# Sixteen conditioning products of a decoder layer, moved from the merge into the mixing stage

## The chip, the cores and the metric

The kernel runs on one core of a Trainium2 chip (trn2). The metric is the device time of one execution in microseconds (us), the median of several runs. Before the change it is 793.3 us.

## The reference

One decoder layer for 512 tokens of width 1024, in float32. A per-sequence vector c conditions it: `mod = silu(c) @ w_ada + b_ada` gives six vectors of 1024 values, shift, scale and gate for each of the two halves of the layer.

```
h = rmsnorm(x, g_pre_mix) * (1 + sc1) + sh1
qa, ka, va, qb, kb, vb, qi, ki, wi, gate_a, gate_b = split(h @ w_in)
mixer a: an indexer picks 128 keys for each query; softmax attention over them
mixer b: stick-breaking attention, a scan over the keys
y = (sigmoid(gate_a) * (oa @ w_up_a) + sigmoid(gate_b) * (ob @ w_up_b)) @ w_out
x = x + ga1 * rmsnorm(y, g_post_mix)
h = rmsnorm(x, g_pre_ffn) * (1 + sc2) + sh2
x = x + ga2 * rmsnorm(relu(h @ w_ff1)**2 @ w_ff2, g_post_ffn)
```

Each mixer has 8 heads of 64. The change concerns two of the six vectors: ga1, the gate of the first half (used after the product with w_out), and sc2, the scale ahead of the MLP.

## The kernel before

Every product with float32 weights is made of three matmuls (`mm3`): weights and activations are each split into a high part (`hi`, by ScalarE, L113) and a low part (`lo`, by VectorE, L114), and high x high, high x low and low x high are summed. A weight tile is 128 x 1024 (512 KB). It is loaded by SyncE's queue into one of three buffers "st" (`stage`, L107 to L110), then split into one of four buffers "whi" and "wlo" (`wload`). Tokens stand in four tiles of 128.

The conditioning vectors are not made by matmuls. w_ada is stored transposed, so that one load of 128 x 1024 (`ada[j]`, j from 0 to 47) holds the weights of 128 outputs. VectorE multiplies it with silu(c), which stands as a row in all partitions (tile "cb"), and sums along the row: `ada_dot` (L213), one column of `mod`. Eight such products make one of the six vectors. `ada_cols(j)` is a load into "st" and this product. For ga1 (j = 16 to 23) and sc2 (j = 32 to 39) a small product with a norm gain follows (`gated_gain`, L134, and `scaled_gain`, L131). `silu_rows(pool)` loads c as a row into "cb" of a pool, takes its sigmoid on ScalarE (L161) and the product on VectorE (L162).

The stages in order of time:

- start (to about 57 us): sh1 and sc1, the first norm, the first tiles of w_in.
- mixing (about 57 to 325 us): `main_stream` makes the remaining projections, and generators (`indexer`, `attend`, `prep_a`) are stepped beside it, one `tick()` for each yield of the main stream, then alone until all are done. A step yields the number of ticks until its next one. The indexer ends with 16 rounds of the 8 largest values (L411, L412) and then writes the mask of selected keys (L416), on which the softmax of mixer a (`rows_a`, L468 to L476) waits.
- merge: for m = 0 to 7, one tile of gate_b (24 matmuls), the two up-projections (24 matmuls, into "s" banks), sigmoids, products and sum on ScalarE and VectorE, and the split of the result. After each m stand `LATE[m]` conditioning products.
- w_out, second norm, and the MLP (w_ff1, then w_ff2 with fewer products by a scheme of sums).

Outside of the start and of the last stage (`manual_schedule`) the order of each engine's queue is not that of the program text: a planner that knows modelled costs orders it ahead of time, and of what its model has ready it takes first what stands first in the text. On the chip each queue is then carried out as ordered. Loads stand on SyncE's queue in the same way.

Pools are stacked: the pool "tmp" (`tp`) of the mixing stage takes the place of the pool of the start stage, and the pool of the merge (`mp`) that of "tmp". The merge has its own `silu_rows(mp)`, so its "cb" is loaded when the mixing is over.

Of the kernel before, what the change touches and what calls it, by code (L numbers as in the profile page):

```python
# [7 lines left out]
F32 = mybir.dt.float32  # L8
# [6 lines left out]
P = 128  # L15
D = 1024
L = 512
NT = L // P
KT = D // P
# [23 lines left out]
A11, S1, S3, S2, A12, A22 = range(6)  # L43
EARLY = 4
WOB = 4
LATE = (0, 3, 4, 4, 4, 4, 4, 1)
HF_ACT = 0
EVAC = 1
EVAC_A = 3
# [16 lines left out]
def layer_kernel(tc, x, ada, vecs, c_row, rope, w_first, w_v, w_b, w_a, w_gate, w_up, w_out, w_ff1, w_ff2, w_right, out):  # L66
    nc = tc.nc
    es = ExitStack()
    with es:
        edge = es.enter_context(tc.tile_pool(name="edge", bufs=1, side="right"))  # L70
        per = es.enter_context(tc.tile_pool(name="per", bufs=1))
# [3 lines left out]
        def uid(name):  # L75
            cnt[0] += 1
            return f"{name}_{cnt[0]}"
# [25 lines left out]
        g2 = per.tile([P, KT], F32, name="g2")  # L103
# [3 lines left out]
        def stage(src, w=D):  # L107
            st = per.tile([P, D], F32, name=uid("st"), tag="st", bufs=3)
            nc.sync.dma_start(st[:, :w], src)
            return st  # L110
# [19 lines left out]
        def scaled_gain(dst, j, g0):  # L130
            nc.vector.scalar_tensor_tensor(dst, mod[:, j:j + 1], 1.0, vec[:, g0:g0 + 1], op0=ALU.add, op1=ALU.mult)  # L131

        def gated_gain(i, j, g0):
            nc.vector.tensor_tensor(ga[:, i:i + 1], mod[:, j:j + 1], vec[:, g0:g0 + 1], op=ALU.mult)  # L134
# [22 lines left out]
        def silu_rows(pool, sg=None):  # L157
            dst = pool.tile([P, D], F32, name=uid("cb"), tag="cb")
            sg = pool.tile([P, D], F32, name=uid("cs"), tag="cs") if sg is None else sg
            nc.sync.dma_start(dst, c_row.to_broadcast([P, D]))  # L160
            nc.scalar.activation(sg, dst, AF.Sigmoid)  # L161
            nc.vector.tensor_tensor(dst, dst, sg, op=ALU.mult)  # L162
            cb[:] = [dst]
# [32 lines left out]
        def slot(name, dt=F32, a=4):  # L196
            t = up.tile([P, 2048], dt, name=uid(name), tag="u8", bufs=6)
            return t.rearrange("p (a b) -> p a b", a=a)
# [13 lines left out]
        def ada_dot(j, st):  # L212
            nc.vector.tensor_tensor_reduce(out=st, in0=st, in1=cb[0], scale=1.0, scalar=vec[:, j:j + 1],  # L213
                                           op0=ALU.mult, op1=ALU.add, accum_out=mod[:, j:j + 1])

        def ada_cols(j):
            ada_dot(j, stage(ada[j]))
# [72 lines left out]
        tp = t_es.enter_context(tc.tile_pool(name="tmp", bufs=1, side="right"))  # L290
# [30 lines left out]
        def k_parts(src):  # L321
            s = tp.tile([P, NT, 3, HD], F32R, name=uid("ks"), tag="ks")
            split(s[:, :, 0, :], s[:, :, 1, :], src)
            nc.scalar.activation(s[:, :, 2, :], s[:, :, 0, :].bitcast(F32), AF.Copy)
            return s
# [7 lines left out]
        def turned(dst, s, i, t0=0):  # L333
            ps = bank("tr", F32R)
            for t in range(t0, NT):
                nc.tensor.transpose(ps[:, t * P:(t + 1) * P], s[:, t, i:i + 2].rearrange("p a d -> p (a d)"), identr)
            evac(dst[:, t0 * P:], ps[:, t0 * P:].bitcast(F32))
# [8 lines left out]
        mask = tp.tile([P, 1280], BF16, name="mask")  # L346
# [7 lines left out]
        tens = {}  # L354

        def spawn(gen, delay=0):
            tasks.append([now[0] + delay, gen])
# [11 lines left out]
        def indexer():  # L369
            do_rope(kw[:, :, None, :HD], 1)  # L370
            s = k_parts(kw[:, :, :HD])
            do_rope(qi[:, :NT - 1].rearrange("p t (h d) -> p t h d", h=NH), NH, 1)
            yield 2
            kk = tp.tile([P, 2, L], F32R, name="kTi")
            for i in range(2):
                turned(kk[:, i], s, i)
            head = lambda h: q_parts(qi[:, :NT - 1, h * HD:(h + 1) * HD])
            s = head(0)
            yield 2
            prev = None  # L380
            for h in range(NH + 1):
                q = None
                if h < NH:
                    q = tp.tile([P, L], F32R, name=uid("qTi"), tag="qTi", bufs=2)
                    turned(q, s, 0, 1)
                    if h + 1 < NH:
                        s = head(h + 1)
                    yield 1
                if prev is not None:
                    for b in range(1, NT):  # L390
                        n = (b + 1) * P
                        ps = scores(prev, kk, b)
                        r = row("rel")
                        nc.scalar.activation(r[:, :n], ps[:, :n], AF.Relu)
                        dst = isc[:, ISC0[b]:ISC0[b] + n]
                        w = kw[:, b, HD + h - 1:HD + h]
                        if h == 1:
                            nc.vector.tensor_scalar(dst, r[:, :n], w, None, op0=ALU.mult)
                        else:
                            nc.vector.scalar_tensor_tensor(dst, r[:, :n], w, dst, op0=ALU.mult, op1=ALU.add)  # L400
                    yield IDX_GAP
                prev = q
            for b in range(1, NT):
                dg = isc[:, ISC0[b] + b * P:ISC0[b] + (b + 1) * P]
                nc.gpsimd.affine_select(out=dg, in_=dg, pattern=[[-1, P]], compare_op=ALU.is_ge,
                                        fill=FILL, base=0, channel_multiplier=1)
            for i in range(TOPK // 8):
                for b in range(1, NT):
                    cur = isc[:, ISC0[b]:ISC0[b] + (b + 1) * P]
                    m8 = small(8)  # L410
                    nc.vector.max(out=m8, in_=cur)  # L411
                    nc.vector.match_replace(out=cur, in_to_replace=m8, in_values=cur, imm_value=SENT)  # L412
                    yield TOP_GAP[b - 1]
            for b in range(1, NT):
                n = (b + 1) * P
                nc.vector.tensor_scalar(mask[:, MSK0[b]:MSK0[b] + n], isc[:, ISC0[b]:ISC0[b] + n],  # L416
                                        -3.3e38, OFF, op0=ALU.is_gt, op1=ALU.mult)
            tens["mask"] = True
# [32 lines left out]
        def attend(key, v_src, rows, lag, gap, close):  # L451
            for hp in range(NH // 2):
                while f"{key}{hp}" not in tens:
                    yield 1
                yield QK_LAG
                pT = [pt_tile(e) for e in range(2)]
                for b in range(NT):
                    spawn(unit(hp, b, tens[f"{key}{hp}"], v_src, rows, pT, lag, close))
                    yield gap[b]
# [19 lines left out]
        def rows_b(q, kk, b):  # L479
# [8 lines left out]
            nc.vector.tensor_tensor(be[:, :n - 1], be[:, :n - 1], a[:, 1:n], op=ALU.mult)  # L488
            return be


        srcs = [(w_v[g, i, :, :(k1 - k0) * VREST], (k1 - k0) * VREST) for g in range(2) for i, (k0, k1) in enumerate(V_CUTS)]
        feeds = {"b": iter(w_b[i] for i in range(8)), "g": iter(w_gate[i] for i in range(8)), "a": iter(w_a[i] for i in range(8))}
# [125 lines left out]

        tens["vb"] = slot("vb")  # L620
        tens["sga"] = [slot("sga") for _ in range(2)]
        spawn(indexer())
        spawn(attend("b", tens["vb"], rows_b, LAG_B, GAP_B, close_b))
        spawn(attend("a", va, rows_a, LAG_A, GAP_A, close_a))
        for _ in main_stream():
# [25 lines left out]
        gsl = slot("mrg")  # L651
        mz = mp.tile([P, LINE // 4], F32, name="mz")[:, 0:1]
        nc.vector.memset(mz, 0.0)
        late = iter([base + k for base in (16, 32, 24) for k in range(KT)])
        for m in range(KT):
            pg = drain(cols_T(wnext()))
            sgb, ta = gsl[:, 2 * (m % 2)], gsl[:, 2 * (m % 2) + 1]
            nc.scalar.activation(sgb, pg, AF.Sigmoid)
            hi, lo = wnext()
            pa, pb = bank("s"), bank("s")  # L660
            for ps, oh, ol, c0 in ((pb, obh, obl, 512), (pa, oah, oal, 0)):
                for k in range(4):
                    cs = slice(c0 + k * P, c0 + (k + 1) * P)
                    mm3(ps, hi[:, cs], lo[:, cs], oh[k], ol[k], k == 0, k == 3)
            nc.vector.tensor_tensor(sgb, pb, sgb, op=ALU.mult)
            sga = tens["sga"][m // 4][:, m % 4]
            nc.scalar.activation(sga, sga, AF.Sigmoid, bias=mz)
            nc.vector.tensor_tensor(ta, pa, tens["sga"][m // 4][:, m % 4], op=ALU.mult)
            nc.vector.tensor_tensor(sgb, sgb, ta, op=ALU.add)
            split(mgh[m], mgl[m], sgb)  # L670
            for _ in range(LATE[m]):
                j = next(late)
                ada_cols(j)
                if j >= 32:
                    scaled_gain(g2[:, j - 32:j - 31], j, 32 + j)
                elif j < 24:
                    gated_gain(j - 16, j, 40 + j)
        u_es.close()
        h_es.close()

# [29 lines left out]
        for k in range(KT):  # L710
            if k < WOB:
                wo.append(wnext())
            else:
                st = stage(w_out[k])
# [410 lines left out]
```

## Time and profile before

| what | value |
|---|---|
| runs | 795.06, 793.3, 790.36 us; median 793.3 us |
| the profiled execution | 792.72 us, of which the span is 790.9 us |
| TensorE (PE) busy | 765.3 us, 97% of the span |
| VectorE (DVE) busy | 593.3 us, 75% |
| ScalarE (ACT) busy | 415.2 us, 53% |
| GpSimd (POOL) busy | 28.2 us, 4% |
| granted TensorE clock | 0.997 |
| conditioning loads into "st" | 32 of 512 KB, of which 24 for the merge |

The span runs from the first to the last instruction of the program. An engine's busy time is the time in which it carries out instructions; "PEld" is TensorE's loading of stationary weights, which overlaps its matmuls. A number after "x" counts instructions. In a timeline, a square bracket gives the idle time of the engine before an instruction and what ended it.

### The profile page before, as it was taken

What the parts mean: (1) busy time and instruction counts of PE and PEld (TensorE: products, weight loads), DVE (VectorE), ACT (ScalarE), POOL (GpSimd) and SP (SyncE); (2) the same over time, 40 slices, a digit from 0 to 9 for tenths busy, and PEclk for the clock granted to TensorE, in tenths of its full rate; (3) what the DMA queues carried; (4) which work ended last, traced back from release to release, by engine and by line L of the source; (5) the groups of instructions that cost most, each with busy time, mean ns of one, the idle gap of its engine ahead of it and who ended that gap; (6) DMA issues with size and microseconds to landing.
All of it is one profiled execution on the core that took longest, in us unless ns stands there. A gap on an engine that the chain in (4) does not pass through costs nothing.

```text
span 790.9 us, 10885 instructions
## 1 busy us (share of the span) xinstructions
PE 765.3 (97%) x4014; PEld 638.5 (81%) x4014; DVE 593.3 (75%) x1112; ACT 415.2 (53%) x752; POOL 28.2 (4%) x44
## 2 busy tenths in 40 slices
PE   6999999998899999999999999999999999999996
PEld 5889978667889877787778898888888878888885
DVE  6876799999966768688875875655645588888966
ACT  6545567654445758632245763232332367768852
POOL 0000000000000000000000000000000011151000
PEclk9999999999999999999999999999999999999999
DMA  9943211113122121177785155344431289899502
GB/s 359 389 122 106 73 37 54 55 53 107 46 89 80 56 65 43 53 249 259 253 278 210 36 187 174 131 139 153 142 105 63 71 202 226 192 208 261 190 1 107
DMA packets 32598, 111.18 MB, mean 141 GB/s; under 512 B 3872, under 2 KB 3872, under 8 KB 32544
## 3 DMA queue, kind: packets, MB, share of 16 engines
q1 hardware_dynamic: 28224, 99.44, 36.2%
q0 software_dynamic: 4176, 11.01, 8.1%
q8 instruction: 31, 0.51, 0.2%
q14 instruction: 23, 0.19, 0.1%
q10 hardware_dynamic: 144, 0.03, 0.0%
HBM read 108.38 MB, written 2.10 MB: 140 GB/s over the span
## 4 chain that ended last, share of the span: by engine, by line
PE 74%; DVE 15%; DMA 6%; ACT 2%; issue 2%; SPq 0%; DVEq 0%; ACTq 0%
PE mm L140 25%; PE s L140 19%; PE o L140 7%; PE s L859 6%; PE mm L859 5%; PE tr L859 5%; DMA st<-in_ada_dram 3%; DVE a L486 3%; DVE wlo L114 2%; DVE isc L412 2%; DVE sm L411 2%; DMA st<-in_w_up_dram 2%; PE tr L430 2%; DVE be L488 1%; PE tr L140 1%
## 5 line engine op out<-in xcount | busy, mean ns | idle before, releaser
L113 ACT ACTIVATE whi<-st 128x1024 fp32r<-128x1024 f32 (+3 forms) x102 | 102.2, 1005 | 161.2 <-DMA st<-in_w_up_dram 43.6
L114 DVE TENSOR_TENSOR wlo<-st,whi 128x1024 fp32r<-128x1024 f32 (+3 forms) x102 | 117.3, 1153 | 55.3 <-ACT whi L113 55.0
L140 PE MATMUL mm<-hTh,whi 128*128 128x512 f32 x192 | 78.2, 407 | 0.1
L140 PE MATMUL mm<-hTh,wlo 128*128 128x512 f32 x192 | 75.3, 392 | 0.0
L140 PE MATMUL mm<-hTl,whi 128*128 128x512 f32 x192 | 75.1, 391 | 0.0
L140 PE MATMUL mm<-whi,hTh 128*128 128x256 f32 (+2 forms) x208 | 62.7, 308 | 0.0
L213 DVE CUSTOM_DVE_ANT_0 st<-st,cb,vec 128x1024 f32<-128x1024 f32 x32 | 40.9, 1283 | 28.6 <-DMA st<-in_ada_dram 28.6
L140 PE MATMUL mm<-wlo,hTh 128*128 128x256 f32 (+2 forms) x208 | 60.6, 297 | 0.0
L140 PE MATMUL mm<-whi,hTl 128*128 128x256 f32 (+2 forms) x208 | 60.5, 297 | 0.0
L140 PE MATMUL s<-h2h,whi 128*128 128x512 f32 (+1 forms) x120 | 43.4, 361 | 0.0
L140 PE MATMUL s<-h2l,whi 128*128 128x512 f32 (+1 forms) x120 | 43.3, 361 | 0.0
L140 PE MATMUL s<-h2h,wlo 128*128 128x512 f32 (+1 forms) x120 | 43.3, 361 | 0.0
L140 PEld LDWEIGHTS mm<-hTh,wlo 128*128 128x128 f32 x192 | 36.0, 188 | 7.7
L140 PEld LDWEIGHTS mm<-hTh,whi 128*128 128x128 f32 x192 | 36.2, 189 | 6.6 <-DVE qT L524 0.3
L140 PEld LDWEIGHTS mm<-hTl,whi 128*128 128x128 f32 x192 | 36.2, 188 | 6.2
L140 PEld LDWEIGHTS mm<-wlo,hTh 128*128 128x128 f32 x208 | 40.1, 193 | 1.1
L140 PEld LDWEIGHTS mm<-whi,hTl 128*128 128x128 f32 x208 | 40.0, 192 | 0.6
L140 PEld LDWEIGHTS mm<-whi,hTh 128*128 128x128 f32 x208 | 39.6, 193 | 0.4
L859 PE MATMUL s<-whi,ah 128*128 128x512 f32 x100 | 36.1, 390 | 0.3 <-ACT whi L113 0.3
L140 PE MATMUL s<-kT,qT 128*128 128x256 f32 (+2 forms) x128 | 30.9, 346 | 2.1 <-ACT be L485 1.8
L879 POOL DMA_DIRECT2D wn<-in_w_right_dram x13 | 11.4, 876 | 582.2 <-DVE ub L898 532.6
L812 DVE TENSOR_TENSOR ub<-ub 128x512 f32<-128x512 f32 (+1 forms) x36 | 22.4, 627 | 10.8 <-ACT ub L811 10.8
(356 smaller groups left out, 1976.1 us busy)
## 6 DMA issues: line engine op xcount, KB each, us to landing
st<-in_w_ff_dram SPq DMA_DIRECT2D x50, 512.0 KB, 3.8
st<-in_ada_dram SPq DMA_DIRECT2D x32, 512.0 KB, 3.9
sa<-in_ada_dram SPq DMA_DIRECT2D x16, 512.0 KB, 8.1
st<-in_w_gate_dram SPq DMA_DIRECT2D x16, 512.0 KB, 3.4
ld<-in_w_ff_dram SPq DMA_DIRECT2D x14, 512.0 KB, 4.7
wn<-in_w_right_dram POOLq DMA_DIRECT2D x13, 512.0 KB, 5.5
st<-in_w_first_dram SPq DMA_DIRECT2D x8, 512.0 KB, 8.5
st<-in_w_b_dram SPq DMA_DIRECT2D x8, 512.0 KB, 3.3
```

Of the source, the lines that this page charges most:

```text
L113: nc.scalar.activation(dst_hi, src, AF.Copy)
L114: nc.vector.tensor_tensor(dst_lo, src, dst_hi.bitcast(F32), op=ALU.subtract)
L140: nc.tensor.matmul(o, lhsT, rhs, start=start, stop=stop)
L213: nc.vector.tensor_tensor_reduce(out=st, in0=st, in1=cb[0], scale=1.0, scalar=vec[:, j:j + 1], op0=ALU.mult, op1=ALU.add, accum_out=mod[:, ...
L411: nc.vector.max(out=m8, in_=cur)
L412: nc.vector.match_replace(out=cur, in_to_replace=m8, in_values=cur, imm_value=SENT)
L430: nc.tensor.transpose(tr[:, j * P:(j + 1) * P], ps[e][:, j * P:(j + 1) * P], ident)
L486: nc.vector.tensor_tensor_scan(a[:, n - 1::-1], a[:, n - 1::-1], zero.to_broadcast([P, n]), 1.0, op0=ALU.mult, op1=ALU.add)
L488: nc.vector.tensor_tensor(be[:, :n - 1], be[:, :n - 1], a[:, 1:n], op=ALU.mult)
L812: nc.vector.tensor_tensor(u, u, u, op=ALU.mult)
L859: nc.tensor.matmul(acc[i], s[:, ts], m[:, cs], start=f, stop=l, skip_group_check=onto)
L879: nc.gpsimd.dma_start(nw[p], w_right[p], accum_op=ALU.add)
```

## The change

Sixteen products, those of ga1 (j = 16 to 23) and sc2 (j = 32 to 39), leave the merge and become a generator of the mixing stage, `late_gains`. It starts when the program text has written the mask; for each k it loads `ada[16 + k]`, makes its product two ticks later, the same for `ada[32 + k]`, and then the two gains. The loads go to a tag of their own, "sad", with two buffers in the pool "tmp". So that silu(c) is there, `silu_rows` is called at the start of the mixing stage, with "cb" in "tmp" and the sigmoid in one of the "st" buffers. The eight products of sh2 (j = 24 to 31) stay in the merge, one for each m. The merge's own `silu_rows(mp)` stays.

```diff
-LATE = (0, 3, 4, 4, 4, 4, 4, 1)
+LATE = (1,) * 8
...
+        def late_gains():
+            while "mask" not in tens:
+                yield 1
+            for k in range(KT):
+                for j in (16 + k, 32 + k):
+                    st = tp.tile([P, D], F32, name=uid("sad"), tag="sad", bufs=2)
+                    nc.sync.dma_start(st, ada[j])
+                    yield 2
+                    ada_dot(j, st)
+                gated_gain(k, 16 + k, 56 + k)
+                scaled_gain(g2[:, k:k + 1], 32 + k, 64 + k)
...
         tens["sga"] = [slot("sga") for _ in range(2)]
+        silu_rows(tp, per.tile([P, D], F32, name="cs0", tag="st", bufs=3))
         spawn(indexer())
+        spawn(late_gains())
...
-        late = iter([base + k for base in (16, 32, 24) for k in range(KT)])
+        late = iter([base + k for base in (24,) for k in range(KT)])
...
             for _ in range(LATE[m]):
-                j = next(late)
-                ada_cols(j)
-                if j >= 32:
-                    scaled_gain(g2[:, j - 32:j - 31], j, 32 + j)
-                elif j < 24:
-                    gated_gain(j - 16, j, 40 + j)
+                ada_cols(next(late))
```

## Rows read from the trace of the kernel before

**Rows 1.** The page: its head and the line of TensorE in part 1.

```profile
span 790.9 us, 10885 instructions
PE 765.3 (97%) x4014; PEld 638.5 (81%) x4014; DVE 593.3 (75%) x1112; ACT 415.2 (53%) x752; POOL 28.2 (4%) x44
```

**Rows 2.** Busy time by stretch; columns as in the first line.

```profile
core 0: us, PE busy (x) PEld busy (x) DVE busy (x) ACT busy (x) POOL busy (x), PEclk, DMA share, GB/s
57.00:100.00 43.00, 43.00 (x300) 41.15 (x299) 30.12 (x67) 25.50 (x58) 0.00 (x0) 1.00 0.26 86
100.00:220.00 120.00, 111.83 (x652) 90.33 (x651) 118.23 (x258) 68.56 (x160) 1.15 (x3) 0.99 0.18 58
219.70:243.70 24.00, 24.00 (x163) 20.18 (x162) 14.01 (x27) 10.84 (x21) 0.00 (x0) 1.00 0.26 88
243.70:330.00 86.30, 86.28 (x553) 71.42 (x552) 60.79 (x189) 61.06 (x146) 0.00 (x0) 1.00 0.17 56
220.00:330.00 110.00, 109.98 (x710) 91.29 (x710) 74.75 (x214) 71.60 (x166) 0.00 (x0) 1.00 0.19 63
336.00:406.00 70.00, 67.19 (x289) 53.38 (x288) 56.92 (x94) 20.01 (x25) 0.00 (x0) 1.00 0.75 253
490.00:590.00 100.00, 100.00 (x443) 82.84 (x442) 54.88 (x89) 27.80 (x36) 0.00 (x0) 1.00 0.42 138
```

**Rows 3.** Timeline of TensorE: start of items 2 and 3, and the merge's end.

```profile
335.91 0.39 PE L140 MATMUL mm<-hTh,whi 128*128 128x512 f32 x1
...
346.79 0.39 PE L140 MATMUL mm<-hTh,whi 128*128 128x512 f32 x1
...
406.08 0.27 PE L154 MATMUL tr<-identr,ga 128*128 128x128 f32 x1
```

**Rows 4.** Waits from 330 to 411 us: total, times, longest.

```profile
ACT whi L113 <- DMA st<-in_w_up_dram: 43.6, 6, 8.6
DVE st L213 <- DMA st<-in_ada_dram: 8.4, 10, 1.7
...
PE s L140 <- DVE wlo L114: 2.1, 4, 0.8
```

**Rows 5.** Timeline of SyncE's queue, 286 to 405 us: start, length, load.

```profile
325.49 0.33 SPq L160 DMA_DIRECT2D cb<-in_c_row_dram  x1
...
361.55 6.39 SPq L109 DMA_DIRECT2D st<-in_ada_dram  x4
369.01 0.33 SPq L109 DMA_DIRECT2D st<-in_w_up_dram  x1
```

**Rows 6.** Timeline of VectorE in the merge: two products in a row.

```profile
366.30 1.28 DVE L213 CUSTOM_DVE_ANT_0 st<-st,cb,vec 128x1024 f32<-128x1024 f32 x1
...
367.62 0.16 DVE L131 SCALAR_TENSOR_TENSOR g<-mod,vec 128x1 f32<-128x1 f32 x1
367.70 1.28 DVE L213 CUSTOM_DVE_ANT_0 st<-st,cb,vec 128x1024 f32<-128x1024 f32 x1
```

**Rows 7.** Groups by line, 325 to 411 us: busy us, mean ns, idle before.

```profile
L213 DVE CUSTOM_DVE_ANT_0 st<-st,cb,vec 128x1024 f32<-128x1024 f32 x24 | 30.6, 1282 | 8.4 <-DMA st<-in_ada_dram 8.4
```

**Rows 8.** Timeline of VectorE, 218 to 247 us: mask, transposes, first softmax row.

```profile
219.06 0.69 DVE L416 TENSOR_SCALAR mask<-isc 128x384 bf16<-128x384 f32 x2
...
227.92 0.69 DVE L187 CAST qT<-tr 128x512 fp32r<-128x512 f32 x1 [2.74 <-PE tr L336]
...
243.76 0.29 DVE L468 CUSTOM_DVE_ANT_0 p<-s,mask 128x128 f32<-128x128 f32 x1
```

**Rows 9.** Timelines: SyncE and ScalarE at the mixing's start; silu in the merge.

```profile
39.02 15.85 SPq L109 DMA_DIRECT2D st<-in_w_v_dram  x6
...
56.41 1.09 ACT L278 ACTIVATE qi<-mm 128x512 f32<-128x512 f32 x2 [2.71 <-PE mm L140]
...
329.22 1.04 ACT L161 ACTIVATE cs<-cb 128x1024 f32<-128x1024 f32 x1
...
330.30 1.23 DVE L162 TENSOR_TENSOR cb<-cb,cs 128x1024 f32<-128x1024 f32 x1 [0.63 <-ACT cs L161]
```

**Rows 10.** Timeline of ScalarE after the merge: split of w_out, k = 4.

```profile
413.62 1.06 ACT L113 ACTIVATE woh<-st 128x1024 fp32r<-128x1024 f32 x1 [1.42 <-DVE mgl L114]
```

## The prediction

> **What bounds the kernel now.** I read the page first, then busy time by stretch, then the merge and the mixing stage one by one. The page shows TensorE busy for nearly the whole span [rows 1]; since matmul ends are modelled, that alone doesn't say it runs at its peak, so I counted matmuls. In the first half of the MLP (490 to 590 us) 443 matmuls fit into 100 us, one per 0.226 us, with TensorE never idle [rows 2]; that is the full rate. The merge (336 to 406 us) falls short of it: 289 in 70 us, with 2.81 us of idle time, while VectorE is busy for 56.92 us of the 70 [rows 2]. Read from TensorE's own rows: one merge item m is 48 matmuls (24 for the gate, 24 for the two up-projections), and an undisturbed one lasts 346.79 - 335.91 = 10.88 us. Items 2 to 7 start at 335.91 and end at 406.08, 70.17 us, where six undisturbed ones would be 65.28 us: **4.89 us are lost** [rows 3].
>
> What loses them: ScalarE waits for the w_up load 6 times for 43.6 us in all, VectorE 10 times for conditioning loads (8.4 us), and then TensorE for the low half of w_up's split [rows 4]. SyncE's queue says why that load is late. Between two weight loads stand four conditioning loads, 361.55 to 367.94, and the next w_up load starts at 369.01 [rows 5]; all of them share the three "st" buffers, so each waits for an earlier VectorE product to free one. And a product takes VectorE 1.40 us from its start to the next one's (366.30 to 367.70, with its 0.16 us gain) [rows 6]; 24 of them were 30.6 us of VectorE in this stage [rows 7].
>
> The mixing stage before it is another case. From 220 to 330 us TensorE is idle for 0.02 us of 110, and VectorE for 110 - 74.75 = 35.25 us [rows 2]. From 100 to 220 us, ahead of the mask, VectorE is busy for 118.23 of 120 us, and there TensorE is idle for 8.17 us [rows 2]. The mask is written at 219.06 us, and the first softmax row of mixer a comes at 243.76 us [rows 8].
>
> **The change, part by part.**
>
> *Out of the merge: 16 of 24 products.* VectorE loses 16 x 1.40 = 22.4 us there, SyncE 16 loads. With one product for each item, VectorE's 56.92 us over 6.4 items (about 8.9 each) become about 5.4 for 10.88 us of matmuls, and three loads instead of six share the "st" buffers per item. What was late is then early by several us, and I see nothing else close behind: the loads of w_out (k = 4 to 7) go to buffers that come free when the merge's last split is done, which moves with the merge [rows 10]. So I take the whole loss: **-4.9 us**. Bounds: -4.9, since TensorE has no more than this to give, and -1.2 if only the share of one of the four late items (4 to 7) goes. [...]
>
> *Into the mixing stage: 16 products of 1.40 us, 22.4 us of VectorE, and 16 loads of 512 KB from SyncE's queue into two "sad" buffers.* What hides them is VectorE's idle time. Of it 24 - 14.01 = 10 us lies between the mask and 243.7 us [rows 2], where VectorE waits for transposes of mixer a's q and k (2.74 us is the longest) and nothing of the softmax stands behind it yet [rows 8]: room for seven products. The other nine, 12.6 us, share the rest up to 330 us, where 86.3 - 60.79 = 25.5 us are idle [rows 2]. A product put into a gap shorter than itself delays the softmax row, the reciprocal or the transpose copy behind it on VectorE by up to 1.2 us; for those wait ScalarE's exponential and TensorE's transposes. With the products VectorE would be busy for (74.75 + 22.4) / 110 = 88%. The nearest row on one side is this stretch itself (68% busy, no TensorE idle time), on the other the merge (81%, 4% idle) and 100:220 (98.5%, 6.8% idle) [rows 2]. The low end is 0 (all in idle time; no gain, since TensorE has 0.02 us of idle time there to give back). The high end is 28 us: nothing covered, and each product also waits 8.4 / 24 = 0.35 us for its load as in the merge [rows 7]. I take +2.0 us, the merge's 4% over the some 50 us in which the nine products stand.
>
> The loads stand on SyncE's queue among weight loads. That queue has long waits without harm in this stretch: the load of c at 325.49 waited behind the last product of mixer a [rows 5], and TensorE still had no idle time. I take 0; if a "sad" load waiting for its product held a weight load past its need, the price is in the third rival.
>
> *New at the start of the mixing: the row of c, its sigmoid (1.04 us of ScalarE) and product (1.23 us of VectorE), as now in the merge [rows 9].* The load has to wait for the buffers of the start stage, then stands on SyncE among the six w_v loads, issued from 39.02 us [rows 9]; its sigmoid uses one of three "st" buffers. VectorE is busy for only 30.12 of the 43 us from 57 to 100 [rows 2], which covers the product; ScalarE idles 2.71 us before 56.41 us [rows 9], which covers the sigmoid. Bounds 0 and 2.3 us (both ops uncovered); I take 0, by the row of 57:100, where TensorE is never idle. The same work stays in the merge for the last eight products, so nothing is saved there.
>
> *The sum:* -4.9 + 2.0 + 0 = -2.9 us against this execution's own 792.72 us (790.9 us of span and 1.8 us around it) is 789.8 us. The median shown is 793.3, over 790.36 to 795.06, so this execution lies 0.6 us under it; I forecast **790 us**.
>
> **The rivals.**
>
> *All covered.* The queue order places the products into gaps as a list does, some even into the 12.9 idle us of 57:100, since they need only c and their loads. Then the sum is -4.9 us: 787.8 us. For it: VectorE's idle time (35 us) is over the need (22.4). Against: what stands behind a product on VectorE waits for its end, whatever it is worth.
>
> *VectorE becomes the bound of the second half.* At 88% it lies between the merge and the stretch ahead of the mask; the line between their idle shares (4% at 81%, 6.8% at 98.5%) gives about 5% of 110 us, 5.6 us, and the sum is +0.7 us: 793.4 us. For it: mixer a's chain goes back and forth between ScalarE and VectorE. Against: TensorE has independent gate products there.
>
> *The other side: products that wait for their loads hold the softmax.* In the merge VectorE stood for a conditioning load at 10 of 24 products [rows 4, 7]. In the mixing stage a product that stands so holds the row maximum and reciprocal behind it, and the end of mixer a moves with it; the merge needs all heads of a before its first sum, so little can be drawn forward. One uncovered product costs 1.40 + 0.35 = 1.75 us. From (4.9 + 4.0) / 1.75, five uncovered ones of 16, the kernel is slower by over 0.5%; at eight it is +14 - 4.9 = +9.1 us: 801.8 us. For it: these waits in the merge, and loads that queue on SyncE behind weight loads. Against: load traffic in this stretch is 63 GB/s where it was 253 in the merge [rows 2], so a load should land before its turn. [...]
>
> *The merge doesn't speed up.* If w_up is late for its buffers and not for the four loads, only the products' own VectorE time goes: -1.2 + 2.0 = +0.8, 793.5 us. Against it speaks the queue: the weight load is issued right behind the four loads, each time [rows 5].
>
> **How the numbers follow.** Forecast (-2.9, its own range -4.5 to -0.5): 0.45. All covered: 0.20. VectorE the bound: 0.13. Waiting products: 0.17. No gain in the merge: 0.05. A change of under 0.5%, 4 us, is about what a measurement of this kernel can tell from none; so faster is below 789.3 us and slower above 797.3. Faster: the covered case and something under half of the forecast, 0.40. Slower: the waiting products and a tail of the bound case, 0.20. The same: 0.40. The range goes from 786.5, a little under the covered case, to 798, which takes in the bound case and five or so uncovered products and leaves out what is worse.
>
> **What would show it.** Right: items 2 to 7 of the merge 10.9 us apart; no wait of ScalarE for w_up of 8 us that ends in a stalled matmul; the products' rows on "sad" mostly between 220 and 300 us or earlier; TensorE's idle time from 220 to 330 us under 2 us, and the last product of mixer a within 2 us of its place (325 us). Wrong: VectorE waiting for "sad" loads by over 5 us in sum, a later end of mixer a, new idle time of TensorE between 57 and 100 us, or merge items still 12 us apart.

## The result, and the profile after

| | median | range of runs | ratio to before, 95% interval |
|---|---|---|---|
| before | 793.41 us | 790.36 to 795.06 (5) | |
| after | 798.72 us | 797.39 to 800.88 (5) | 1.0071 [1.0053, 1.0089] |

The change makes the kernel slower by 0.71%, 5.6 us. The forecast was 790 us, the range ended at 798. Ratios here and below are of undisturbed executions; a single one is left out by that, 2421.68 us in e9. The profiled execution of after took 799.86 us, of which the span is 798.1 us.

The page of after, its head and TensorE's line (before: [rows 1]):

```profile
span 798.1 us, 10902 instructions
PE 766.4 (96%) x4014; PEld 641.3 (80%) x4014; DVE 592.3 (74%) x1113; ACT 416.1 (52%) x753; POOL 28.2 (4%) x44
```

TensorE has the same 4014 matmuls and is busy 1.1 us longer in a span that is 7.2 us longer. Where the rest is lost shows in busy time by stretch, after (columns as in [rows 2]):

```profile
57.00:100.00 43.00, 38.07 (x257) 36.81 (x256) 37.99 (x89) 24.03 (x52) 0.00 (x0) 0.92 0.68 229
62.00:66.00 4.00, 2.58 (x10) 2.34 (x11) 4.00 (x7) 2.31 (x5) 0.00 (x0) 0.65 0.50 149
66.00:70.00 4.00, 4.00 (x19) 4.00 (x18) 3.25 (x9) 0.40 (x2) 0.00 (x0) 0.50 0.94 347
100.00:220.00 120.00, 112.20 (x632) 89.33 (x631) 118.67 (x251) 69.92 (x160) 1.15 (x3) 0.99 0.23 75
220.00:336.00 116.00, 113.54 (x757) 95.55 (x756) 87.19 (x249) 70.28 (x169) 0.00 (x0) 1.00 0.21 69
346.83:412.12 65.29, 65.29 (x290) 54.02 (x289) 38.23 (x49) 19.43 (x26) 0.00 (x0) 1.00 0.53 176
```

Three readings. First, from 57 to 100 us, where before had no idle time and 300 matmuls, after has 4.93 us of idle time and 257, and from 66 to 70 us TensorE is busy all the time but does 19 matmuls in 4 us: its granted clock is 0.50 there. Second, from 220 to 336 us there are 2.46 us of idle time, where before has 0.02 from 220 to 330 [rows 2]. Third, over items 2 to 7 of the merge (the last row) TensorE has none left, and VectorE is busy for 38.23 us of 65.29, where before has 57.01 of 70.17.

TensorE's rows of after: the front (from here on: the start of the mixing, with the added row of c), then items 2 and 3 and the end of the merge (before: [rows 3]):

```profile
58.10 0.39 PE L140 MATMUL tr<-whi,hTl 128*128 128x512 f32 x1
62.24 0.53 PE L140 MATMUL mm<-whi,hTh 128*128 128x292 f32 x2 [3.75 <-ACT whi L113]
63.96 0.61 PE L140 MATMUL mm<-wlo,hTh 128*128 128x292 f32 x1 [1.19 <-DVE wlo L114]
...
346.83 0.39 PE L140 MATMUL mm<-hTh,whi 128*128 128x512 f32 x1
...
357.71 0.39 PE L140 MATMUL mm<-hTh,whi 128*128 128x512 f32 x1
...
412.12 1.03 PE L154 MATMUL tr<-identr,ga 128*128 128x128 f32 x8
```

The merge is as forecast: items 2 to 7 take 412.12 - 346.83 = 65.29 us, six times 10.88, where before took 70.17: **4.88 us gained**. But item 2 starts at 346.83 instead of 335.91, **10.92 us late**. So the question is what those 10.9 us are. The front shows two waits, 4.94 us in sum, for the split of a weight tile. Which, SyncE's queue says, and ScalarE's rows (before: [rows 9]):

```profile
51.17 0.33 SPq L160 DMA_DIRECT2D cb<-in_c_row_dram  x1
51.55 0.90 SPq L497 DMA_DIRECT2D sad<-in_ada_dram  x2
52.50 7.01 SPq L109 DMA_DIRECT2D st<-in_w_v_dram  x3
```

```profile
55.54 1.28 ACT L161 ACT_TABLE_LOAD   x1 [5.12 <-DMA cb<-in_c_row_dram]
56.84 1.06 ACT L161 ACTIVATE cs<-cb 128x1024 f32<-128x1024 f32 x1
...
61.24 2.35 ACT L113 ACTIVATE whi<-st 128x876 fp32r<-128x876 f32 x3
```

Before, the six w_v loads were issued from 39.02 us. Now the first starts at 52.50, behind the row of c and two "sad" loads, and the row of c waits until 51.17 for the buffers of the start stage, whose room "cb" takes (SyncE waits 11.6 us there for VectorE's hTl). In before ScalarE splits three w_v tiles at 45.26, 47.76 and 53.01 us, ahead of the copies of qi and va out of TensorE's banks (from 56.41 us). In after it stands 5.12 us for the row, loads a table for the sigmoid (1.28 us), makes these copies, and comes to the first w_v split at 61.24 us; TensorE, idle from 58.49 us, goes on at 62.24.

And the products are not where the text puts them. Groups of VectorE's instructions in after, 57 to 115 us and then 115 to 340 us, and its timeline at the mask and the first softmax row (before: [rows 8]):

```profile
L213 DVE CUSTOM_DVE_ANT_0 sad<-sad,cb,vec 128x1024 f32<-128x1024 f32 x13 | 16.6, 1279 | 1.0 <-DMA sad<-in_ada_dram 1.0
...
L213 DVE CUSTOM_DVE_ANT_0 sad<-sad,cb,vec 128x1024 f32<-128x1024 f32 x3 | 3.8, 1278 | 0.0
```

```profile
230.03 0.69 DVE L416 TENSOR_SCALAR mask<-isc 128x384 bf16<-128x384 f32 x2
230.63 1.28 DVE L213 CUSTOM_DVE_ANT_0 sad<-sad,cb,vec 128x1024 f32<-128x1024 f32 x1
...
254.61 0.29 DVE L468 CUSTOM_DVE_ANT_0 p<-s,mask 128x128 f32<-128x128 f32 x1
```

Thirteen of the sixteen stand ahead of the mask, between 61.63 and 111.19 us, on the engine that is full from 100 to 220 us (118.67 of 120); the rows of the mask come at 230.03 instead of 219.06, the first softmax row at 254.61 instead of 243.76. That is 10.97 and 10.85 us late, as late as item 2. So by the time the mask is written the whole loss is there; the experiments part the front from the products.

### The profile page after: what moved, and what is told of

It reads as the page before. It is cut to its first block, busy times and chain, and to the rows that moved or that the text cites. A ratio compares the mean times of both kernels' runs of the same rounds, so it can differ in the third digit from the quotient of the medians.

```text
span 798.1 us, 10902 instructions
## 1 busy us (share of the span) xinstructions
PE 766.4 (96%) x4014; PEld 641.3 (80%) x4014; DVE 592.3 (74%) x1113; ACT 416.1 (52%) x753; POOL 28.2 (4%) x44
## 4 chain that ended last, share of the span: by engine, by line
PE 75%; DVE 18%; issue 3%; ACT 3%; DMA 2%; DVEq 0%; SPq 0%; ACTq 0%
PE mm L140 25%; PE s L140 22%; PE s L868 6%; PE o L140 6%; PE mm L868 5%; PE tr L868 5%; DVE wlo L114 3%; DVE isc L412 3%; DVE a L486 2%; DVE sm L411 2%; DVE be L488 2%; PE o L868 1%; PE tr L140 1%; PE tr L430 1%; DVE isc L400 1%
## 5 line engine op out<-in xcount | busy, mean ns | idle before, releaser
L213 DVE CUSTOM_DVE_ANT_0 st<-st,cb,vec 128x1024 f32<-128x1024 f32 x16 | 20.6, 1284 | 28.2 <-DMA st<-in_ada_dram 28.0
L821 DVE TENSOR_TENSOR ub<-ub 128x512 f32<-128x512 f32 (+1 forms) x36 | 22.4, 626 | 10.9 <-ACT ub L820 10.9
```

The lines of the kernel that those rows point to most:

```text
L821: nc.vector.tensor_tensor(u, u, u, op=ALU.mult)
```

## The experiments

Each was timed beside the kernel before on the same chip. The chip was not the same for all (e1 to e4, e5 to e8, e9 to e11 and e12 each had one of their own), so compare the ratios rather than the medians. In "row kept" variants the row silu(c), which the start stage makes for its own 16 products, goes into a small pool of its own instead of that stage's pool and is used again; then no `silu_rows(tp)` is needed:

```diff
+        k_es = ExitStack()
+        keep = k_es.enter_context(tc.tile_pool(name="keep", bufs=1, side="right"))
...
-        cb.append(sp.tile([P, D], F32, name="cb"))
+        cb.append(keep.tile([P, D], F32, name="cb"))
```

| run | median us | ratio to before, 95% interval |
|---|---|---|
| e1_row_kept | 793.21 | 1.0003 [0.9991, 1.0015] |
| e2_front_alone | 800.09 | 1.0083 [1.0061, 1.0105] |
| e3_own_sigmoid | 792.87 | 1.0002 [0.9991, 1.0012] |
| e4_eight_moved | 790.05 | 0.9967 [0.9953, 0.9981] |
| e5_held16 | 790.88 | 0.9971 [0.9959, 0.9982] |
| e6_eight_one_row | 788.97 | 0.9951 [0.9935, 0.9968] |
| e7_held8 | 790.29 | 0.9972 [0.996, 0.9984] |
| e8_even | 798.84 | 1.0076 [1.0056, 1.0097] |
| e9_even_ga_last | 798.51 | 1.008 [1.0066, 1.0094] |
| e10_even_one_row | 788.72 | 0.9954 [0.994, 0.9967] |
| e11_held16_one_row | 789.89 | 0.997 [0.9957, 0.9983] |
| e12_early_row | 787.01 | 0.9935 [0.992, 0.995] |

**The front, e1 to e3.** e1 is after with the row kept and without `silu_rows(tp)`:

> The sixteen products stay moved, but silu(c) is not loaded again at the start of the mixing: the row made at the start stays in a buffer of its own until the merge is over. Theory A (the row of c at the mixing's start holds the value weights and costs 7.9 us): 798.7 - 7.9 = 790.8 us, no idle time of TensorE at 58 us. Theory B (the products in the mixing cost about 10 us of VectorE's time, the start next to nothing): 797.5 to 798.7 us, and the mask is still written at about 230 us.

e2 is the opposite: before, with only that call added. Its row is used by nothing.

```diff
+        silu_rows(tp, per.tile([P, D], F32, name="cs0", tag="st", bufs=3))
         spawn(indexer())
```

> The kernel before, with the row of c loaded and turned to silu at the start of the mixing as in the changed kernel, and no product moved (the row is not used). Theory A: 793.4 + 7 to 8 = 800.4 to 801.4 us, with TensorE idle for about 5 us at 58 us and a lower granted clock after it. Theory B: at most 794.5 us.

e3 is after with one word changed, the ring from which the sigmoid's buffer is taken:

```diff
-        silu_rows(tp, per.tile([P, D], F32, name="cs0", tag="st", bufs=3))
+        silu_rows(tp, tp.tile([P, D], F32, name="cs0", tag="sad", bufs=2))
```

> The changed kernel with one edit: the sigmoid of the row of c stands in one of the two sad buffers, not in one of the three st buffers; the row is still loaded at the start of the mixing. Theory A, if it is the shared st buffer that puts the value weights behind the row of c: the value weights are issued from 39 us on again, and the time is 791 to 792 us. Theory A, if it is the load of the row itself and its sigmoid on ScalarE: 797 to 798.7 us. Theory B: 798 us.

e2 alone costs 0.83%, 6.6 us; taking the call away (e1) or only its "st" buffer (e3) gives back 1.0071 - 1.0002 = 0.69%, 5.5 us. So nearly all of it is neither the row of c nor its sigmoid nor its product, but the buffer. SyncE's queue of e3:

```profile
39.49 12.22 SPq L109 DMA_DIRECT2D st<-in_w_v_dram  x5
51.98 0.33 SPq L160 DMA_DIRECT2D cb<-in_c_row_dram  x1
55.17 0.33 SPq L109 DMA_DIRECT2D st<-in_w_v_dram  x1
```

and of e2:

```profile
50.00 0.33 SPq L160 DMA_DIRECT2D cb<-in_c_row_dram  x1
50.42 13.73 SPq L109 DMA_DIRECT2D st<-in_w_v_dram  x6
```

The "st" buffers are given out in the order of the text. If the sigmoid has one of them, every w_v load, later in the text, gets its buffer after it; the sigmoid needs the row, the row waits for the room of the start stage until 50 or 51 us, and the queue has all six weight loads behind it. With the sigmoid elsewhere five of them pass, and TensorE is busy at a granted clock of 1.00 in the two stretches of 4 us. From 57 to 100 us it still has 1.75 us of idle time, for ScalarE's copies of qi behind the sigmoid; e1, without the row, has 1.21 us, and the two kernels don't differ in time. e3, by stretch:

```profile
57.00:100.00 43.00, 41.25 (x290) 39.33 (x289) 39.17 (x91) 26.37 (x57) 0.00 (x0) 1.00 0.65 212
62.00:66.00 4.00, 4.00 (x34) 4.00 (x34) 2.92 (x7) 2.94 (x8) 0.00 (x0) 1.00 0.47 136
66.00:70.00 4.00, 4.00 (x32) 4.00 (x32) 4.00 (x9) 0.84 (x3) 0.00 (x0) 1.00 0.73 251
```

Without the front, the change is worth nothing (e1 and e3, 0.2 us; both lie above the 790.8 to 792 us that I expected), though the merge gains its 4.9 us there too: in e3 items 2 to 7 start 10.88 us apart. So the mixing stage costs about 5 us. The mask's rows of e2 and e3 (before 219.06 [rows 8], after 230.03), and how late three points are against before, in us:

```profile
226.27 0.69 DVE L416 TENSOR_SCALAR mask<-isc 128x384 bf16<-128x384 f32 x2
222.14 0.69 DVE L416 TENSOR_SCALAR mask<-isc 128x384 bf16<-128x384 f32 x2
```

| run | mask | first softmax row | item 2 |
|---|---|---|---|
| after | 10.97 | 10.85 | 10.92 |
| e2, the front alone | 7.21 | 5.88 | 5.88 |
| e3, the products alone | 3.08 | 4.56 | 4.53 |
| e1, the products alone | 3.54 | 6.15 | 6.14 |
| e5, products held behind the mask | 0.96 | 3.73 | 3.59 |
| e6, eight products | 3.17 | 1.91 | 1.13 |
| e7, eight products held | 0.64 | 3.30 | 2.35 |

The front and the products add up: 5.88 + 4.53 = 10.41 of 10.92 us at item 2. And the products cost at two places. Those drawn ahead of the mask delay it by 3.1 to 3.5 us; kernels here that move nothing have it between 0.3 us earlier and 1.2 later than before. The four (e1) to six (e3) that stay behind it put another 1.5 to 2.6 us between mask and softmax.

**Where the products stand, e4 to e7 and e11.** e5 is e1 with the products tied to the mask: each sum starts from its bias in b_ada, and that bias now comes from a tile that is computed from the mask (0 x mask + b_ada), so that none can be ordered ahead of it.

```diff
+            vg = tp.tile([P, 32], F32, name="vg")
+            nc.vector.scalar_tensor_tensor(vg, mask[:, MSK0[3]:MSK0[3] + 32], 0.0, vec[:, 16:48], op0=ALU.mult, op1=ALU.add)
...
-                    ada_dot(j, st)
+                    nc.vector.tensor_tensor_reduce(out=st, in0=st, in1=cb[0], scale=1.0, scalar=vg[:, j - 16:j - 15],
+                                                   op0=ALU.mult, op1=ALU.add, accum_out=mod[:, j:j + 1])
```

> As e1 (row kept, sixteen products moved), but each product also reads a small tile that is made from the finished mask, so none can stand ahead of the mask in VectorE's queue. Theory H (in e1 eleven products stood between 57 and 110 us, ahead of the mask, in a stretch where VectorE is full soon after, and so the mask came 3.5 us later): the mask is back at 218 to 219 us, and with the idle time behind it the mixing costs about 2 us: 790.4 us. Theory G (a product costs about 0.3 us wherever it stands in the mixing): 793 us as e1.

e4 keeps the row and moves ga1's eight products only; sc2's stay in the merge, two products for each m. e6 is e4 without the second row, `silu_rows(mp)`; e7 is e6 with the eight tied to the mask; e11 is e5 without the second row.

```diff
-LATE = (1,) * 8
+LATE = (2,) * 8
...
-                for j in (16 + k, 32 + k):
+                for j in (16 + k,):
...
-        silu_rows(mp)
```

> As e1 (the row kept), but only the eight products of ga1 are moved, and the merge keeps two per item. Theory A, with 2 us for sixteen products in the mixing: the merge still loses nothing (VectorE busy for about 6.8 of 10.88 us per item), the mixing costs half, 793.4 - 4.9 + 1.2 = 789.7 us. Theory B (about 10 us for sixteen): 793.4 - 4.9 + 5 = 793.5 us.

> As e4 (row kept, eight products moved, two per item in the merge), and the merge uses the kept row too: no second load of c, no second sigmoid and product. If these are hidden in the merge: 790 us as e4. If the first merge items wait for them (the load stood on SyncE's queue for 15 us behind the end of mixer a): 788.5 to 789.5 us.

> As e6, but the eight products are held behind the mask as in e5. Theory H: eight products of 1.4 us, 11.2 us, meet 10 us of idle time between mask and softmax and cost 0 to 0.5 us: 793.4 - 4.9 + 0.3 = 788.8 us. Theory G: as e6.

> As e5 (row kept, sixteen products held behind the mask), and the merge uses the kept row. e6 stood 1.1 us under e4 by this edit: 789.8 us. If it is hidden with one product per item: 790.9 us as e5.

Holding sixteen behind the mask gains 0.32% against e1 (1.0003 to 0.9971, the intervals apart). Busy time of e5 from 220 to 330 us, and TensorE's waits from 218 to 300 us:

```profile
220.00:330.00 110.00, 107.95 (x694) 89.25 (x693) 93.11 (x264) 67.73 (x162) 0.00 (x0) 0.98 0.38 125
```

```profile
PE tr L338 <- DVE ks L114: 1.2, 1, 1.2
PE tr L338 <- DVE qT L187: 0.9, 1, 0.9
```

All sixteen lie from 220.96 to 276.94 us, VectorE is at 85%, and TensorE stands for 2.05 us, all of it early, for transposes of mixer a's q and k behind products. That is the place that I had forecast, and near the price (2.6 us for 2.0). But the stretch between mask and softmax is not free room, as I had it: with eight of the products there the softmax is 3.73 us late.

With eight, the tie gains nothing (e7 over e6, 0.9951 to 0.9972, the intervals overlap; I had expected 788.8 us and got 790.29). The table says why: it gives back the mask's delay, and the products are then in the softmax's way. Why eight delay the mask at all is open. They stand from 58 to 84 us and take 8 x 1.40 = 11.2 us, and VectorE had 12.9 idle us from 57 to 100 [rows 2], so room alone doesn't say it.

What the second row costs is not clear of noise: e6 against e4 is 0.9967 to 0.9951 with overlapping intervals, e11 against e5 0.9971 to 0.9970.

**The merge itself, e8 to e10 and e12.** e8 moves nothing out and only evens the share, three products for each m; e9 is e8 with ga1's eight last; e10 is e9 with the row kept and no `silu_rows(mp)`.

```diff
-LATE = (0, 3, 4, 4, 4, 4, 4, 1)
+LATE = (3,) * 8
...
-        late = iter([base + k for base in (16, 32, 24) for k in range(KT)])
+        late = iter([base + k for base in (32, 24, 16) for k in range(KT)])
```

> The kernel before with nothing moved to the mixing: all 24 products stay in the merge, three after each item and not up to four. If the late w_up load behind four others is what costs 4.9 us, three loads per item leave it in time for most items and the gain is 3 to 4 us: 789.5 to 790.5 us. If it is VectorE's 24 products as a whole, they cost the same as before: 793 us.

> The kernel before, nothing moved: three products after each merge item, as e8, but in the order sc2, sh2, ga1, so that the transposes of ga1 can't stand in TensorE's queue before the merge is over (in e8 they stood before item 2 and TensorE idled about 8 us there). If four loads in a row ahead of the w_up load are what costs the merge 4.9 us: items 2 to 7 are 10.9 us apart and the time is 788.0 to 789.5 us. If e8's full-rate items were a gift of the 8 us idle ahead of them (buffers filled meanwhile): items 12 us apart at the end and 792 to 793 us.

> As e9, and the row of silu(c) made at the start is kept until the end of the merge, so the merge loads no second one. As e9 if that row is hidden: within 0.7 us of it; 1 to 2 us less if the early products can now run in the mixing's idle time.

e8 and e9 are slower than before, by 0.8%, where I had expected a gain or at worst no change, though their items 2 to 7 are 10.88 us apart with three products each. TensorE and SyncE's queue in e9:

```profile
330.17 0.39 PE L140 MATMUL mm<-hTh,wlo 128*128 128x512 f32 x1
337.23 0.80 PE L140 MATMUL s<-obh,whi 128*128 128x512 f32 x1 [6.66 <-ACT whi L113]
```

```profile
324.95 0.33 SPq L160 DMA_DIRECT2D cb<-in_c_row_dram  x1
332.82 0.33 SPq L109 DMA_DIRECT2D st<-in_w_up_dram  x1
```

Three conditioning tiles hold the three "st" buffers, their products wait for a row that is loaded at 324.95 us, after the mixing, and the next w_up load stands behind them until 332.82: 6.66 us of idle time. In e8 it is 5.7 us in three pieces (not 8, as I wrote ahead of e9), the longest for the transposes of ga1. With the row there from the start (e10) it is gone, and the kernel gains. My reason for e8's and e9's design, that four products in an item are what loses, needed a last test: e12 is before with the row kept and without `silu_rows(mp)`, and nothing else; no product is moved and LATE is as before.

```diff
-        silu_rows(mp)
```

> The kernel before, with the row silu(c) of the start kept and no second one in the merge; LATE = (0, 3, 4, 4, 4, 4, 4, 1) and its order stay, nothing is moved. It parts the gain of e10 (ratio 0.9954, 788.7 us) into the even share of products and the row that is there early. Theory A, the merge loses because four products stand in an item: with the row alone items 4 to 7 keep their 11.5 to 12.5 us, the gain is at most the second row's 1.1 us, ratio 0.998 to 1.000 (791 to 792.5 us). Theory B, the row is what counts: once the products do not wait for a row loaded after the mixing, the first of them are drawn into the mixing stage, the merge runs at 10.9 us per item, and the ratio is 0.995 to 0.996 (788.5 to 789.5 us) with four products per item as well.

**787.01 us, ratio 0.9935: faster than before and after, and the lowest time of all kernels here** (its interval overlaps those of e6 and e10). Its waits from 330 to 411 us, busy time over items 2 to 7 (e12, then before), its TensorE rows, and SyncE's w_up loads (for items 2, 3, 6 and 7):

```profile
ACT whi L113 <- DMA st<-in_w_up_dram: 36.7, 5, 10.1
```

```profile
333.67:398.95 65.28, 65.28 (x290) 54.02 (x289) 52.46 (x84) 20.24 (x28) 0.00 (x0) 1.00 0.77 255
335.91:406.08 70.17, 67.36 (x290) 53.46 (x288) 57.01 (x94) 20.09 (x25) 0.00 (x0) 1.00 0.75 254
```

```profile
333.67 0.39 PE L140 MATMUL mm<-hTh,whi 128*128 128x512 f32 x1
344.55 0.39 PE L140 MATMUL mm<-hTh,whi 128*128 128x512 f32 x1
...
398.95 1.03 PE L154 MATMUL tr<-identr,ga 128*128 128x128 f32 x8
```

```profile
308.56 0.33 SPq L109 DMA_DIRECT2D st<-in_w_up_dram  x1
...
312.47 18.41 SPq L109 DMA_DIRECT2D st<-in_ada_dram  x4
331.69 0.33 SPq L109 DMA_DIRECT2D st<-in_w_up_dram  x1
...
369.46 0.33 SPq L109 DMA_DIRECT2D st<-in_w_up_dram  x1
...
381.59 0.33 SPq L109 DMA_DIRECT2D st<-in_w_up_dram  x1
```

and the same loads in before (290.58: the conditioning tiles; 333.36: item 2; 382.07 and 394.15: items 6 and 7):

```profile
290.58 19.70 SPq L109 DMA_DIRECT2D st<-in_ada_dram  x3
...
333.36 0.33 SPq L109 DMA_DIRECT2D st<-in_w_up_dram  x1
...
382.07 0.33 SPq L109 DMA_DIRECT2D st<-in_w_up_dram  x1
394.15 0.33 SPq L109 DMA_DIRECT2D st<-in_w_up_dram  x1
```

In e12 ScalarE still waits 36.7 us for w_up, VectorE is as busy as before (52.46 of 65.28 us, 80%, against 57.01 of 70.17, 81%), the traffic is the same (255 against 254 GB/s), a round of loads still takes 12 us (369.46 to 381.59; before 382.07 to 394.15) for an item of 10.88, and yet TensorE has no idle time. What differs is the lead. In before item 2's w_up load comes 335.91 - 333.36 = 2.55 us ahead of the item, and each slow round eats of it: item 7's comes 0.36 us after its item's start (393.79). In e12 it is 333.67 - 308.56 = 25.1 us at item 2, and 388.07 - 381.59 = 6.5 us are left at item 7. So four products in an item do not by themselves make the merge lose; it lost because its loads started with too little lead. Two things go together in that early start, and e12 doesn't part them: in before the three conditioning tiles that stand ahead of item 2's load wait for the late row of c and hold the "st" buffers, and in e12 they are done early, with three more; so six products, not three, stand ahead of item 2, and 18 are left in items 2 to 7.

## Why the prediction was wrong

**The step that failed is "New at the start of the mixing", for which I took 0, with bounds 0 and 2.3 us; it measured 5.5 us (after against e3) to 6.6 us (e2 alone).** I priced its two instructions by their durations, and in the same sentence wrote that the load stands among the six w_v loads and that the sigmoid uses one of three "st" buffers. The two together are the mechanism, and I didn't follow them: which loads get their buffer after the sigmoid, and what those are for. Its price is not that of the instructions but of 4.9 us in which TensorE stands, and of a granted clock of 0.50 behind it (66 to 70 us). (The sigmoid was also underpriced: at this place it has a table load of 1.28 us ahead of it, and ScalarE stands 5.12 us for the row.) My list of what would make the prediction wrong had two signs that came, new idle time between 57 and 100 us and a later end of mixer a; no rival had the mechanism.

**The mixing term, +2.0, was mis-sized: it measured about 5** (e1 and e3: 0.2 = -4.9 + 5.1). I took the text's place for the products, behind the mask, and there the price was near: e5 is -2.3 us, that is -4.9 + 2.6. But nothing in the data ties a product to the mask, and in the covered rival I had noted that the queue's order draws them forward, as a gain. Drawn ahead of it, eight to twelve of them delay the mask by 2.5 to 3.5 us (e4, e6, e3, e1); and the idle 10 us behind the mask, which I counted as free for seven, are not: the softmax comes another 1.5 to 2.6 us later.

**The merge term, -4.9, was right** (70.17 to 65.29 us), and so the rival without it falls. That w_up stands behind four loads was read rightly; that fewer loads are needed was not, by e12: the same four loads do no harm with a lead. And the load of c at 325.49 us, which I took for a long wait without harm, is what leaves the merge without that lead.

**The other rivals.** The waiting products' 801.8 us is nearer to the result than my forecast, but not by its mechanism: VectorE waited for "sad" loads once, 1.0 us in all. VectorE as the bound of the second half was priced at 5.6 us; with all sixteen products there (e5) it was 2.6.

**The sum as measured:** -4.9 (merge) + 5.0 (mixing) + 5.5 (front) = +5.6 us. What stays open: the front and the products were each taken out alone, and e3 against after gives the front by difference. How far the two act on each other is not known better than this: by the medians the parts taken alone come to 1.1 us more than the whole, at item 2 to 0.5 us less. The mixing term as a time is known to about 1 us only: at item 2 it is 4.5 us in e3 and 6.1 in e1.

## What to carry to other kernels

When an edit takes a buffer of an existing ring, list who gets the next buffers of that ring and what they feed: the wait of the newcomer becomes theirs, and the durations of its own instructions say nothing of that price. The place of work in the text is not its place in the queue; look for what in the data could hold it there, and price it where it will be drawn. Where loads come in rounds that are a little slower than the work, ask first how much lead they start with: an input that is ready earlier may do what moving the work was meant to do.

## What was not expected of the hardware

After 4.94 us of idle time in two pieces (58.5 to 64.0 us) TensorE's granted clock was 0.65 from 62 to 66 us and 0.50 from 66 to 70 us, with TensorE busy for all of the latter four: 19 matmuls, where e3 did 32 in the same four microseconds at a granted clock of 1.00. In e2, too, which has 4.34 us of idle time from 57 to 100 us, the clock is 0.50 from 62 to 66 us and 0.70 from 66 to 70 us. The wait there cost more than its length: item 2 of e2 is 5.88 us late. In after TensorE is busy without a break from 66 to 100 us (34.00 of 34 us), and the granted clock is 1.00 from 70 to 74 us. A lower clock follows the 6.66 us of idle time in e9 as well: from 330 to 340 us the granted clock is 0.68 there, and the matmul behind the wait lasts 0.80 us, the one ahead of it 0.39.
